# A 4096-cubed matrix product with leaky ReLU: the first unit of k in two runs of 512, A's first run ahead of B, 16-bit transposes

## The chip, the cores and the metric

One core of one Trainium2 chip. The metric is the device time of one execution in microseconds (us); medians are of 4 to 9 executions. "Granted clock" is the share of full speed that the profile records for TensorE. Time ahead of its first record counts as 1.00 in the views and in the mean clock of a run, though the matmuls there start 0.427 us apart, at half pace: a clock of 1.000 says that it did not fall later, not when it became full.

## The reference

```python
def reference(a, b, alpha):          # a, b: 4096 x 4096 float32, alpha 0.01
    x = np.matmul(a, b)
    return np.where(x > 0, x, alpha * x)
```

## The kernel before: the parts that matter

Both operands are rounded to bf16; a matmul multiplies 128 rows of A by 512 columns of B over 128 values of k. 8192 of them are needed. Eight PSUM banks hold four row tiles (`mt`) times two column halves (`nt`). k is cut in four units of 1024; a step is the work on one unit for half of the rows. From the second step on, GpSimd's loads cast while they copy and VectorE turns A. The first unit is special, because nothing has been loaded yet: it comes as fp32 by SP's queue, TensorE transposes A, and ScalarE and VectorE round both operands on the way.

```python
order = [("a", 0), ("b", 0), ("a", 1), ("b", 1), ("a", 2), ("b", 2), ("a", 3)]
order += [("b", c) for c in range(3, kc0)]             # each 512 KB
...
def turn_a(i):
    cols = a_in[:, i, :].rearrange("m (p c) -> m c p", c=kc0)
    for c in range(kc0):                               # 8 fp32 transposes
        nc.tensor.transpose(turned[i, 2 * c // kc0][:, c % (kc0 // 2), :], cols[:, c, :], ident)
    for half, copy in ((0, nc.scalar.copy), (1, nc.vector.tensor_copy)):
        ...                                            # out of PSUM, to bf16
def round_b(i):
    for nt, copy in ((0, nc.scalar.copy), (1, nc.vector.tensor_copy)):
        copy(b0[:, i, columns(nt)], b_in[i][:, columns(nt)])
...
if (what, i) == ("b", 2):                              # lets GpSimd start the next step's loads
    nc.gpsimd.tensor_copy(x[:, :1], b0[:, 2, :1])
```

Ahead of all that, 8 matmuls on zeros ("fillers") run while the first loads are under way, and 2 more after the first tile's transposes.

## Time and profile before

| | before |
|---|---|
| time, median of 6 | 1785.2 us (1784.67 to 1785.49) |
| span of the profile | 1783.2 us |
| TensorE busy | 1768.7 us, 99% (164 matmul records are missing) |
| first real matmul | 6.74 us |
| VectorE's first copy out of a finished bank | 24.79 us |
| last bank's activation starts | 1779.65 us |

How to read it: TensorE is never the idle engine after some 15 us, so the time is the fixed pace of 8192 matmuls plus what is lost ahead of that. VectorE's first copy out of a finished bank tells when the first unit ends; a change in it goes to the end of the kernel one for one unless a later wait takes it up. The profile's lines for this stand in the prediction.

### The profile page before, as it was taken

Reading aid. Unit: us, or ns where it says so; the run is one execution under the profiler, and the core shown is the slowest. Engines: PE = TensorE matmul, PEld = TensorE weight load, DVE = VectorE, ACT = ScalarE, POOL = GpSimd, SP = SyncE. Lnnn points to the kernel's source line nnn. Section 1 sums busy time; section 2 is a strip of 40 time slices with the busy share of each in tenths; the row PEclk is TensorE's granted clock in tenths of the full one; section 3 lists DMA queues with packets and bytes.
Section 4 is the critical chain, followed back from the end, with each engine's and each line's share of the span. In section 5 each row is a group of like instructions: output and inputs, shape, how many; then the busy total and the mean of one; then the engine's idle time right before and its main releaser. Section 6 shows DMA issues by size and latency. Waiting matters only on the chain.

```text
span 1783.2 us, 17975 instructions
## 1 busy us (share of the span) xinstructions
PE 1768.7 (99%) x8070; PEld 806.6 (45%) x8234; DVE 153.4 (9%) x117; ACT 152.0 (9%) x270; POOL 360.1 (20%) x663
## 2 busy tenths in 40 slices
PE   9999999999999999999999999999999999999999
PEld 4444444444444444444444444444444444444444
DVE  4530000032000000002200000000220000000000
ACT  2010000000000000000000000000000000000001
POOL 4630210433002020043201202014320110301000
PEclk9999999999999999999999999999999999999999
DMA  9994653987139165397704917449860481835511
GB/s 260 195 252 108 115 133 86 190 127 125 40 94 189 48 119 118 94 198 128 124 25 96 188 48 142 94 103 202 128 121 12 112 171 48 165 72 121 115 48 47
DMA packets 147020, 214.06 MB, mean 120 GB/s; under 512 B 12800, under 2 KB 76288, under 8 KB 146944
## 3 DMA queue, kind: packets, MB, share of 16 engines
q0 software_dynamic: 126208, 139.50, 48.3%
q10 hardware_dynamic: 18000, 65.54, 9.4%
q1 hardware_dynamic: 2736, 7.87, 1.2%
q8 instruction: 64, 1.05, 0.2%
q14 instruction: 12, 0.10, 0.0%
HBM read 285.21 MB, written 67.11 MB: 198 GB/s over the span
## 4 chain that ended last, share of the span: by engine, by line
PE 99%; issue 1%; DMA 0%; ACT 0%; SPq 0%; DVE 0%
PE ps L154 99%; DMA a_in<-in_a_dram 0%; PE turned L268 0%; DVE at L271 0%; ACT o L384 0%; ACT at L271 0%; SPq L253 0%; SPq L251 0%
## 5 line engine op out<-in xcount | busy, mean ns | idle before, releaser
L154 PE MATMUL ps<-bt,at 128*128 128x512 bf16 x8028 | 1760.5, 379 | 9.3 <-ACT bt L275 0.3
L154 PEld LDWEIGHTS <-at 128*128 128x128 bf16 x8192 | 801.4, 98 | 967.3 <-ACT at L271 1.3
L138 POOL DMA_DIRECT2D bt<-in_b_dram x408 | 217.1, 539 | 1084.7 <-PE ps L154 893.5
L384 ACT ACTIVATE o<-ps 128x512 f32<-128x512 f32 x240 | 130.7, 595 | 1524.5 <-PE ps L154 1450.8
L121 DVE STREAM_TRANSPOSE at<-a 128x1024 uint32<-128x1024 uint32 (+1 forms) x63 | 123.0, 1986 | 1135.7 <-PE ps L154 1113.8
L116 POOL DMA_DIRECT2D a<-in_a_dram x248 | 142.1, 579 | 203.4 <-DVE at L121 140.1
L231 DVE TENSOR_TENSOR part<-ps,part 128x512 f32<-128x512 f32 x32 | 20.4, 686 | 32.6 <-PE ps L154 32.6
L234 ACT ACTIVATE o<-part 128x1024 f32<-128x1024 f32 x8 | 8.5, 1057 | 77.0 <-DVE part L231 64.2
L229 ACT COPY part<-ps 128x512 f32<-128x512 f32 x8 | 4.4, 593 | 15.1 <-PE ps L154 12.3
L227 DVE COPY part<-ps 128x512 f32<-128x512 f32 x8 | 5.2, 679 | 4.8 <-PE ps L154 4.8
L268 PEld LDWEIGHTS turned<-ident,a_in 128*128 128x128 f32 x32 | 4.3, 196 | 2.4 <-issue 1.2
L268 PE MATMUL turned<-ident,a_in 128*128 128x128 f32 x32 | 4.8, 296 | 0.4 <-DMA a_in<-in_a_dram 0.4
L275 ACT CAST bt<-b_in 128x512 bf16<-128x512 f32 x8 | 5.0, 619 | 2.2 <-DMA b_in<-in_b_dram 2.1
L84 PE MATMUL ps<-w 128*128 128x512 bf16 x8 | 3.6, 631 | 1.2 <-DVE x L80 1.2
L275 DVE CAST bt<-b_in 128x512 bf16<-128x512 f32 x8 | 3.4, 432 | 3.8 <-DMA b_in<-in_b_dram 3.8
L271 DVE CAST at<-turned 128x512 bf16<-128x512 f32 x4 | 2.8, 692 | 10.5 <-PE turned L268 10.5
L271 ACT CAST at<-turned 128x512 bf16<-128x512 f32 x4 | 2.3, 585 | 8.7 <-PE turned L268 8.7
L311 POOL CAST x<-bt 128x1 f32<-128x1 bf16 x1 | 0.3, 348 | 11.1 <-ACT bt L275 11.1
L84 PEld LDWEIGHTS <-w 128*128 128x128 bf16 x8 | 1.0, 140 | 2.8 <-issue 1.7
L81 ACT ACT_TABLE_LOAD x1 | 1.3, 1283 | 0.7 <-PEq L406 0.7
L297 PE MATMUL ps<-w 128*128 128x512 bf16 x2 | 0.6, 379 | 0.0
L78 DVE MEMSET w<- 128x256 uint32 x1 | 0.3, 272 | 0.9 <-PEq L406 0.9
(9 smaller groups left out, 1.4 us busy)
## 6 DMA issues: line engine op xcount, KB each, us to landing
bt<-in_b_dram POOLq DMA_DIRECT2D x408, 256.0 KB, 7.9
out_dram<-o ACTq DMA_DIRECT2D x125, 512.0 KB, 3.1
a<-in_a_dram POOLq DMA_DIRECT2D x248, 128.0 KB, 5.2
b_in<-in_b_dram SPq DMA_DIRECT2D x7, 512.0 KB, 10.0
a_in<-in_a_dram SPq DMA_DIRECT2D x4, 512.0 KB, 7.0
out_dram<-o SPq DMA_DIRECT2D x6, 256.0 KB, 2.0
b_in<-in_b_dram SPq DMA_DIRECT2D x2, 256.0 KB, 10.4
```

The source lines that it names most:

```text
L84: nc.tensor.matmul(wp, w[:, :P], w, start=True, stop=True)
L116: nc.gpsimd.dma_start(to, src.rearrange("(g i) w -> i g w", i=32))
L121: nc.vector.transpose(dst.rearrange("p c m e -> p c (m e)").bitcast(U32) .rearrange("p c (g i) -> p g c i", i=32), held[0][:, 4 * t0:4 * t ...
L138: nc.gpsimd.dma_start(new_b(pi, u)[:, c0 + c, :], b_rows(n, s, c))
L154: nc.tensor.matmul(ps, plain(t)[:, c, rows] if (mb, h, u) == (0, 0, 0) else t[:, c // 2, rows, c % 2], bt[pi, u][:, c, nt * NT:(nt + 1) * NT],
L227: nc.vector.tensor_copy(kept, banks[mt, nt])
L231: nc.vector.tensor_add(kept, banks[mt, nt], kept)
L234: nc.scalar.activation(o, part[h][:, mt, :], LRELU, alpha=alpha)
L268: nc.tensor.transpose(turned[i, 2 * c // kc0][:, c % (kc0 // 2), :], cols[:, c, :], ident)
L271: copy(plain(a0)[:, c:c + kc0 // 2, i * P:(i + 1) * P], turned[i, half])
L275: copy(b0[:, i, columns(nt)], b_in[i][:, columns(nt)])
L384: nc.scalar.activation(o[:, cols], banks[mt, nt], LRELU, alpha=alpha)
```

## The change

Its intent: let every chunk of B find all four row tiles of A, so that TensorE gets work faster than chunks land, and make the transposes cheaper. A's first run of 512 k leads in four loads of 256 KB; A's second run comes between B's chunks. VectorE rounds A first, so that transposes are 16-bit. No bank is free for the second run's transposes, so the bank of the last tile and half (`ps7`) is held back for them, and its early products are made up after B's fifth chunk. The next step's A comes in two runs too, and its loads start after B's fourth chunk instead of the third. The last tiles' stores are merged as well. The core of the diff (load helpers, bank tags and bookkeeping are cut):

```diff
-SEGS = [(0, 0, 8), (1, 0, 8), (2, 0, 8), (3, 0, 8)]
+RUNS = [2, 1, 1, 1]
...
-    order = [("a", 0), ("b", 0), ("a", 1), ("b", 1), ("a", 2), ("b", 2), ("a", 3)]
-    order += [("b", c) for c in range(3, kc0)]
+    order = [("a", 0, 0, 1), ("a", 1, 0, 1), ("a", 2, 0, 1), ("a", 3, 0, 1)]
+    order += [("b", 0), ("b", 1), ("b", 2), ("a", 0, 1, 2), ("b", 3), ("a", 2, 1, 2)]
+    order += [("b", c) for c in range(4, KC)]
...
+    def turn_a(i, r, tiles):
+        nc.vector.tensor_copy(a_rounded[:, i:i + tiles, k], a_in[:, i:i + tiles, k])
+        tag = "ps7" if r else f"ps{4 + i}"
+        turned = psum_pool.tile([P, per, tiles, P], BF16, name="turned", tag=tag)
...
+        if r:
+            leaving.append(lambda: nc.vector.tensor_copy(to, turned))
+        else:
+            nc.scalar.copy(to, turned)
...
+            if n < 3:
+                nc.tensor.matmul(wp, w[:, :P], w, start=True, stop=True)
...
-        if (what, i) == ("b", 2):
+        if (what, i) == ("b", 3):
-            nc.gpsimd.tensor_copy(x[:, :1], b0[:, 2, :1])
+            nc.gpsimd.tensor_copy(x[:, :1], b0[:, 3, :1])
+        if (what, i) == ("b", 4):
+            open_bank["late"] = True
+            for c in late:
+                mm0(MT - 1, c, NP - 1)
```

More of the change, by code (lines that the diff above doesn't have):

```diff
@@ L58 @@
     NB = N // RN
-    assert TURNS[0] == [0] and sorted(sum(TURNS, [])) == list(range(len(SEGS)))
-    assert sum(kc for _, _, kc in SEGS) * P == K
-    SEGS_OF = [[s for s in range(len(SEGS)) if SEGS[s][0] == u] for u in range(KU)]
+    KW = KC * P
+    assert TURNS[0] == [0] and sum(TURNS, []) == list(range(KU)) and len(RUNS) == KU
     small_pool = ctx.enter_context(tc.tile_pool(name="small", bufs=1))
@@ L68 @@
     o_pool = ctx.enter_context(tc.tile_pool(name="oo", bufs=2))
-    psum_pool = ctx.enter_context(tc.tile_pool(name="psum", bufs=8, space=bass.MemoryType.PSUM))
-    ident = small_pool.tile([P, P], FP32, name="ident")
+    psum_pool = ctx.enter_context(tc.tile_pool(name="psum", bufs=1, space=bass.MemoryType.PSUM))
+    ident = small_pool.tile([P, P], BF16, name="ident")
     make_identity(nc, ident)
@@ L81 @@
     nc.scalar.activation(x, x, LRELU, alpha=alpha)
-    wp = psum_pool.tile([P, NT], FP32, name="ps")
+    wp = psum_pool.tile([P, NT], FP32, name="wp", tag="ps3")
     for _ in range(8):
@@ L97, in new_b, with load_a @@
         return bt[pi, u]
-    def k_of(s):
-        u, c0, kc = SEGS[s]
-        return (u * KC + c0) * P, kc * P
-    def load_a(mb, h, s, mt, tiles):
-        u, c0, kc = SEGS[s]
-        k0, kw = k_of(s)
+    def load_a(mb, h, u, mt, r):
+        tiles = 2 * RUNS[u]
+        kw = KW // RUNS[u]
+        kc = kw // P
+        k0 = u * KW + r * kw
         row = ((mb * HALVES + h) * MT + mt) * P
@@ L119, in turn @@
         def turn(t0=0, t1=tiles):
-            dst = new_a(mb, h, u)[:, c0 // 2:(c0 + kc) // 2, (mt + t0) * P:(mt + t1) * P, :]
+            rows = slice((mt + t0) * P, (mt + t1) * P)
+            dst = new_a(mb, h, u)[:, r * kc // 2:(r + 1) * kc // 2, rows, :]
             nc.vector.transpose(
@@ L128, in load_a, with b_rows, load_b, pieces_a @@
         return fetch, turn
-    def b_rows(n, s, c):
-        k0, kw = k_of(s)
-        src = b[k0:k0 + kw, n * RN:(n + 1) * RN]
-        return src.rearrange("(p c) n -> p c n", p=P)[:, c, :]
-    def load_b(pi, n, s, c):
-        u, c0, _ = SEGS[s]
-        nc.gpsimd.dma_start(new_b(pi, u)[:, c0 + c, :], b_rows(n, s, c))
-    def pieces_a(mb, h, s, tiles=None):
-        tiles = tiles or 2 * KC // SEGS[s][2]
-        return [load_a(mb, h, s, mt, tiles) for mt in range(0, MT, tiles)]
-    def pieces_b(pi, s):
-        return [lambda c=c: load_b(pi, pairs[pi], s, c) for c in range(SEGS[s][2])]
+    def b_rows(n, u, c):
+        per = KC // RUNS[u]
+        k0 = u * KW + c // per * per * P
+        src = b[k0:k0 + per * P, n * RN:(n + 1) * RN]
+        return src.rearrange("(p c) n -> p c n", p=P)[:, c % per, :]
+    def load_b(pi, n, u, c):
+        nc.gpsimd.dma_start(new_b(pi, u)[:, c, :], b_rows(n, u, c))
+    def pieces_a(mb, h, u):
+        return [load_a(mb, h, u, mt, r) for mt in range(0, MT, 2 * RUNS[u])
+                for r in range(RUNS[u])]
+    def pieces_b(pi, u):
+        return [lambda c=c: load_b(pi, pairs[pi], u, c) for c in range(KC)]
     def plain(t):
@@ L160, in mm, with new_bank @@
         )
+    def new_bank(mt, nt):
+        return psum_pool.tile([P, NT], FP32, name="ps", tag=f"ps{NP * mt + nt}")
     def new_banks():
         return {
-            (mt, nt): psum_pool.tile([P, NT], FP32, name="ps")
+            (mt, nt): new_bank(mt, nt)
             for mt in range(MT)
@@ L188 @@
             lead = 2 if pi == 1 else KU
-            for s in SEGS_OF[u]:
-                loads.setdefault(first * KU + u - lead, []).extend(pieces_b(pi, s))
+            loads.setdefault(first * KU + u - lead, []).extend(pieces_b(pi, u))
     for mb in range(1, MB):
@@ L194 @@
             for u in range(KU):
-                for s in SEGS_OF[u]:
-                    at_slot = first * KU + h * KU + u - 2 * KU + 1
-                    for fetch, turn in pieces_a(mb, h, s):
-                        loads.setdefault(at_slot, []).extend([fetch, turn])
+                at_slot = first * KU + h * KU + u - 2 * KU + 1
+                for fetch, turn in pieces_a(mb, h, u):
+                    loads.setdefault(at_slot, []).extend([fetch, turn])
     def quarter_of(pieces, quarter):
@@ L205 @@
     steps = [
-        (t, h, s, i == 0, i == len(turn) - 1)
+        (t, h, u, i == 0, i == len(turn) - 1)
         for t, turn in enumerate(TURNS)
         for h in range(HALVES)
-        for i, s in enumerate(turn)
+        for i, u in enumerate(turn)
     ]
@@ L214 @@
     turns = []
-    for i, (_, h, s, _, _) in enumerate(steps):
-        made = pieces_a(0, h, s, 2 if i == 1 else None) if i else []
-        fetches.append([fetch for fetch, _ in made] + (pieces_b(0, s) if i and h == 0 else []))
+    for i, (_, h, u, _, _) in enumerate(steps):
+        made = pieces_a(0, h, u) if i else []
+        fetches.append([fetch for fetch, _ in made] + (pieces_b(0, u) if i and h == 0 else []))
         turns.append([turn for _, turn in made])
@@ L235, in spill @@
             nc.scalar.dma_start(place(0, h, pairs[0], mt), o)
-    kw0 = k_of(0)[1]
-    kc0 = SEGS[0][2]
-    a_in = bt_pool.tile([P, MT, kw0], FP32, name="a_in", tag="bt")
-    b_two = [part_pool.tile([P, kc0 // 2, RN], FP32, name="b_in", tag="part") for _ in range(2)]
-    b_in = [b_two[c // 4][:, c % 4, :] for c in range(kc0)]
-    order = [("a", 0), ("b", 0), ("a", 1), ("b", 1), ("a", 2), ("b", 2), ("a", 3)]
-    order += [("b", c) for c in range(3, kc0)]
+    runs = RUNS[0]
+    per = KC // runs
+    rw = per * P
+    assert runs == 2
+    a_rounded = at_pool.tile([P, MT, KW], BF16, name="a_rounded", tag="at")
+    a_in = bt_pool.tile([P, MT, KW], FP32, name="a_in", tag="bt")
+    b_two = [part_pool.tile([P, KC // 2, RN], FP32, name="b_in", tag="part") for _ in range(2)]
+    b_in = [b_two[c // 4][:, c % 4, :] for c in range(KC)]
+    order = [("a", 0, 0, 1), ("a", 1, 0, 1), ("a", 2, 0, 1), ("a", 3, 0, 1)]
+    order += [("b", 0), ("b", 1), ("b", 2), ("a", 0, 1, 2), ("b", 3), ("a", 2, 1, 2)]
+    order += [("b", c) for c in range(4, KC)]
+    HALVED = (KC - 1,)
     def columns(nt):
         return slice(nt * NT, (nt + 1) * NT)
-    for what, i in order:
+    for what, i, *more in order:
         if what == "a":
-            nc.sync.dma_start(a_in[:, i, :], a[i * P:(i + 1) * P, :kw0])
-        elif i < kc0 - 1:
+            r, tiles = more
+            k = slice(r * rw, (r + 1) * rw)
+            src = a[i * P:(i + tiles) * P, k].rearrange("(t p) k -> p t k", p=P)
+            nc.sync.dma_start(a_in[:, i:i + tiles, k], src)
+        elif i not in HALVED:
             nc.sync.dma_start(b_in[i], b_rows(pairs[0], 0, i))
@@ L258 @@
     b0 = new_b(0, 0)
-    turned = {
-        (i, half): psum_pool.tile([P, kc0 // 2, P], FP32, name="turned", tag="ps")
-        for i in range(MT)
-        for half in range(2)
-    }
-    def turn_a(i):
-        cols = a_in[:, i, :].rearrange("m (p c) -> m c p", c=kc0)
-        for c in range(kc0):
-            nc.tensor.transpose(turned[i, 2 * c // kc0][:, c % (kc0 // 2), :], cols[:, c, :], ident)
-        for half, copy in ((0, nc.scalar.copy), (1, nc.vector.tensor_copy)):
-            c = half * kc0 // 2
-            copy(plain(a0)[:, c:c + kc0 // 2, i * P:(i + 1) * P], turned[i, half])
+    leaving = []
+    def turn_a(i, r, tiles):
+        k = slice(r * rw, (r + 1) * rw)
+        nc.vector.tensor_copy(a_rounded[:, i:i + tiles, k], a_in[:, i:i + tiles, k])
+        tag = "ps7" if r else f"ps{4 + i}"
+        turned = psum_pool.tile([P, per, tiles, P], BF16, name="turned", tag=tag)
+        cols = a_rounded[:, :, k].rearrange("m t (p c) -> m t c p", c=per)
+        for t in range(tiles):
+            for c in range(per):
+                nc.tensor.transpose(turned[:, c, t, :], cols[:, i + t, c, :], ident)
+        to = plain(a0)[:, r * per:(r + 1) * per, i * P:(i + tiles) * P]
+        turned = turned.rearrange("p c t m -> p c (t m)")
+        if r:
+            leaving.append(lambda: nc.vector.tensor_copy(to, turned))
+        else:
+            nc.scalar.copy(to, turned)
     def round_b(i):
@@ L275, in round_b @@
             copy(b0[:, i, columns(nt)], b_in[i][:, columns(nt)])
+        for leave in leaving:
+            leave()
+        leaving.clear()
     there = {"a": [], "b": []}
     waiting = []
-    begun = set()
+    late = []
     banks = {}
-    def work():
-        for mt, c in waiting:
-            for nt in range(NP):
-                mm(banks[mt, nt], 0, 0, 0, 0, mt, nt, c, (mt, nt) not in begun, False)
-                begun.add((mt, nt))
-        waiting.clear()
-    for n, (what, i) in enumerate(order):
-        if what == "a":
-            turn_a(i)
+    open_bank = {"late": False}
@@ new lines, in mm0, with work @@
+    def mm0(mt, c, nt, stop=False):
+        if (mt, nt) == (MT - 1, NP - 1) and not open_bank["late"]:
+            late.append(c)
+            return
+        started = (mt, nt) in banks
+        if not started:
+            banks[mt, nt] = new_bank(mt, nt)
+        mm(banks[mt, nt], 0, 0, 0, 0, mt, nt, c, not started, stop)
+    def work(keep=0):
+        now = waiting[:len(waiting) - keep]
+        del waiting[:len(now)]
+        for nt in range(NP):
+            for mt, c in now:
+                mm0(mt, c, nt)
@@ L293 @@
+    for n, (what, i, *more) in enumerate(order):
+        if what == "a":
+            r, tiles = more
+            turn_a(i, r, tiles)
+            if n < 3:
+                nc.tensor.matmul(wp, w[:, :P], w, start=True, stop=True)
+            work()
+            there["a"] += [(i + t, r) for t in range(tiles)]
+            waiting += [(i + t, c) for t in range(tiles) for c in there["b"] if c // per == r]
         else:
             round_b(i)
-        if n == 0:
-            for _ in range(2):
-                nc.tensor.matmul(wp, w[:, :P], w, start=True, stop=True)
-            banks = new_banks()
@@ L299 @@
-        work()
-        there[what].append(i)
-        if what == "a":
-            waiting += [(i, c) for c in there["b"]]
-        elif n < len(order) - 1:
-            waiting += [(mt, i) for mt in there["a"]]
-            kept = waiting.pop() if len(waiting) > 1 else None
-            work()
-            if kept:
-                waiting.append(kept)
-        if (what, i) == ("b", 2):
-            nc.gpsimd.tensor_copy(x[:, :1], b0[:, 2, :1])
-        if n == len(order) - 1:
-            part[0] = part_pool.tile([P, MT, RN], FP32, name="part", tag="part")
@@ L314 @@
-    waiting += [(mt, kc0 - 1) for mt in there["a"]]
+            work()
+            there["b"].append(i)
+            waiting += [(mt, i) for mt, r in there["a"] if i // per == r]
+            if n < len(order) - 1:
+                work(keep=1)
+        if (what, i) == ("b", 3):
[4 more added lines that the diff above has]
+                mm0(MT - 1, c, NP - 1)
+    part[0] = part_pool.tile([P, MT, RN], FP32, name="part", tag="part")
@@ L318 @@
         for mt, c in waiting:
-            mm(banks[mt, nt], 0, 0, 0, 0, mt, nt, c, False, True)
+            mm0(mt, c, nt, stop=c == KC - 1)
     turns[1][0](0, 1)
@@ L324 @@
             turns[1][0](1, 2)
+    turns[1][0](2, 4)
     turns[1][1]()
@@ L329 @@
     for i in range(1, len(steps)):
-        t, h, s, first, last = steps[i]
-        u, c0, kc = SEGS[s]
-        head = 0 if h else kc // 2 if last else kc
+        t, h, u, first, last = steps[i]
+        head = 0 if h else KC // 2 if last else KC
         groups = [([(mt, c) for c in range(head) for mt in range(MT)], None)]
-        groups += [([(mt, c) for c in range(head, kc)], mt if last else None) for mt in range(MT)]
+        if i == 1:
+            head = KC // RUNS[u]
+            groups = [([(mt, c) for mt in range(MT) for c in range(head)], None)]
+        groups += [([(mt, c) for c in range(head, KC)], mt if last else None) for mt in range(MT)]
         following = turns[i + 1] if i + 1 < len(steps) else []
-        if len(following) == 1:
-            where = [2]
-        else:
-            where = [0, 3]
+        where = [0, 3]
         own = 2 * KU - 2 + i - (len(steps) - 2)
@@ L355 @@
                 for nt in range(NP):
-                    mm(banks[mt, nt], 0, h, 0, u, mt, nt, c0 + c, first and c == 0,
-                       last and c == kc - 1)
+                    mm(banks[mt, nt], 0, h, 0, u, mt, nt, c, first and c == 0,
+                       last and c == KC - 1)
             for piece, turn in enumerate(following):
@@ L384 @@
                         nc.scalar.activation(o[:, cols], banks[mt, nt], LRELU, alpha=alpha)
-                        if final and mt:
+                        if final and mt == MT - 1:
                             nc.sync.dma_start(to[:, cols], o[:, cols])
-                    if not final or mt == 0:
+                    if not final or mt < MT - 1:
                         nc.scalar.dma_start(to, o)
```

## The prediction

> **What bounds the kernel now.** I read the page first (engine shares, the chain that ended last, the groups), then the timeline of the first 40 us and of the last 10, then the issue and landing times of the DMAs. The page says that TensorE is the bound, and that one line of the kernel is nearly the whole chain:
>
> ```profile
> span 1783.2 us, 17975 instructions
> ...
> PE 1768.7 (99%) x8070; PEld 806.6 (45%) x8234; DVE 153.4 (9%) x117; ACT 152.0 (9%) x270; POOL 360.1 (20%) x663
> ...
> PE 99%; issue 1%; DMA 0%; ACT 0%; SPq 0%; DVE 0%
> ...
> L154 PE MATMUL ps<-bt,at 128*128 128x512 bf16 x8028 | 1760.5, 379 | 9.3 <-ACT bt L275 0.3
> L154 PEld LDWEIGHTS <-at 128*128 128x128 bf16 x8192 | 801.4, 98 | 967.3 <-ACT at L271 1.3
> L268 PE MATMUL turned<-ident,a_in 128*128 128x128 f32 x32 | 4.8, 296 | 0.4 <-DMA a_in<-in_a_dram 0.4
> ```
>
> The reader is to see two things. The product takes 8192 matmuls (the weight loads count them; 164 matmul records are missing). And 379 ns is the latency of one, not its pace: in the chain in order of time, stretches begin at 23.87 and at 34.66 us and hold 50 matmuls, so the pace is 10.79 / 50 = 0.2158 us. 8192 x 0.2158 = 1767.9 us that the change doesn't touch. The rest of the span is 1783.2 - 1767.9 = 15.3 us, and it lies at the two ends. The last bank's activation starts at 1779.65, so 3.55 us are the way out of the last tile; about 11.7 us are lost at the front. TensorE's timeline shows where:
>
> ```profile
> 4.58 1.41 PE L268 MATMUL turned<-ident,a_in 128*128 128x128 f32 x8
> 5.83 0.59 PE L297 MATMUL ps<-w 128*128 128x512 bf16 x2
> 6.74 0.75 PE L154 MATMUL ps<-bt,at 128*128 128x512 bf16 x2 [0.32 <-ACT bt L275]
> 7.84 1.16 PE L268 MATMUL turned<-ident,a_in 128*128 128x128 f32 x8 [0.36 <-DMA a_in<-in_a_dram]
> 9.23 0.94 PE L154 MATMUL ps<-bt,at 128*128 128x512 bf16 x3 [0.23 <-ACT at L271]
> 9.79 0.70 PE L154 MATMUL ps<-bt,at 128*128 128x512 bf16 x2
> 10.49 1.13 PE L268 MATMUL turned<-ident,a_in 128*128 128x128 f32 x8
> 11.46 2.11 PE L154 MATMUL ps<-bt,at 128*128 128x512 bf16 x9
> 13.62 1.05 PE L268 MATMUL turned<-ident,a_in 128*128 128x128 f32 x8
> 14.51 25.71 PE L154 MATMUL ps<-bt,at 128*128 128x512 bf16 x115
> ```
>
> The first real matmul is at 6.74; then three batches of fp32 transposes and small waits for A and B alternate with matmuls; from about 15.4 on the starts follow each other at 0.2158 us with no gap to the end. By the moment at which the first unit's banks come free (DVE's first copy out at 24.79), I put the end of the first unit (64 matmuls, 13.8 us of work) at 25.2 us. So **the quantity to predict is this one**: 25.2 - 13.8 = 11.4 us of front, and any stall that the change makes right after it.
>
> **What the Trainium skill says.** "TensorE: Matmul & The Clock Gate", section on the back-to-back gap, gives 215.7 ns for 512 columns at the full clock: the trace agrees (215.8). The same page, in "Why this matters for your kernels", warns of idle gaps over some 3 us, after which the clock halves; the page's granted clock is full from 5.3 us, and nothing in this trace shows a fall. "DMA: Bandwidth & Descriptors", Specifications, asks for at least 512 B per transfer for line rate. The DMA packet records agree as far as they go: 4096 B packets take about 161 ns, 2048 B ones 93 ns (so 12 to 16% more per byte), 512 B ones on the software queue 60 ns with overlap; smaller data packets do not occur. "VectorE: DVE Perf Modes", tier table, allows at most double rate for a PSUM source; the fp32 copies here (512 elements in 0.69 us) run at single rate, and no 16-bit one occurs.
>
> **The change, part by part.**
>
> 1. *Order of loads.* Before, A tile, B chunk, A tile, B chunk, each 512 KB, landed at 4.4, 5.6, 7.8, 9.1 and then every 1.28 us. Now four half-length A tiles of 256 KB come ahead of the first B chunk: 1.5 MB instead of 1 MB must land before the first product, and A's rows become 2 KB packets. Working from the landings: third slot 7.8, plus 0.1 to 0.4 for the smaller packets, is B0 at about 7.9 to 8.2 (7.1 if the 0.9 us that the third landing lost is not lost again). ACT's cast takes 0.62, so the first real matmul comes at about 8.5 (7.9 to 8.9) instead of 6.74. **Cost: about +1.8 us.**
>
> 2. *Transposes.* 32 of fp32, 0.111 us apart when warm, become 32 of bf16, which I put at 0.055 to 0.08. Before, 24 of them stood among the matmuls (2.7 us); now 16 do (0.9 to 1.3), the first 16 fall into the wait for B0. **Gain: 1.4 to 1.8 us.** The new rounding of A on DVE costs 0.42 us for 512 columns (as B's cast) and about 0.69 for 1024, beside TensorE.
>
> 3. *Work per chunk.* Once four A tiles are there, each B chunk brings 8 matmuls, 1.73 us, against 1.28 us to land it. Before, the first chunks brought 2, 4, 10, and TensorE waited. Of the 11.4 us of front, 6.74 is before the first product and 2.7 are transposes, so about 1.9 are waits. Now I walk the chunks: 8.6 first product; B0, B1, B2 give seven each (one bank is withheld) to 12.9 without a wait; A's second run 12.0 + 0.69 rounding, transposes to 13.4; B3 lands about 13.3, cast by 13.95, wait 0.2, done 15.3; A's other half lands 14.75, rounded by 15.45, wait 0.3, transposed and left over by 16.4; B4 lands 16.0, cast by 16.65, wait 0.3; its third tile waits 0.1 more for DVE's copy out of the last bank. 36 matmuls are left and chunks come faster than work: 36 x 0.2158 = 7.8, **end of the unit near 24.6**. If the 0.9 us is not lost, 23.9. The waits now sum to 0.9, **gain about 1.0**. Together: +1.8 - 1.6 - 1.0 = -0.8, and I take 24.4 against 25.2.
>
> 4. *The withheld bank.* Its four early matmuls are done after B4; the number of matmuls is the same. No cost unless DVE's copy (about 0.67 us at double rate, 1.2 at single) is late.
>
> 5. *The next step's A.* GpSimd starts its loads when B3 is rounded instead of B2: 14.0 against 12.4. These too are cut in two runs, so the packets written become 256 B. Before, four issues from 12.67 landed by 22.08 and DVE turned the first tile at 22.20, with 1.5 us to spare before the first copy out:
>
> ```profile
> 22.20 1.10 DVE L121 STREAM_TRANSPOSE at<-a 128x512 uint32<-128x512 uint32 x1 [0.93 <-DMA a<-in_a_dram]
> 24.79 0.69 DVE L227 COPY part<-ps 128x512 f32<-128x512 f32 x1 [1.48 <-PE ps L154]
> 25.39 1.10 DVE L121 STREAM_TRANSPOSE at<-a 128x512 uint32<-128x512 uint32 x1
> 26.42 1.85 DVE L227 COPY part<-ps 128x512 f32<-128x512 f32 x3
> ```
>
> Now 1 MB from about 18.0 (software packets came 4 us after issue), beside the last 0.3 MB of B, at 400 GB/s and 1.4 us to land, is 22.7; with packets up to half as efficient, 25.1. A quarter-size turn is about 0.67 us, and the copy that frees the second bank stands behind it on DVE. With a landing at 23.4: turned 24.1, bank freed 24.7, wanted at about 24.6. Later the third and fourth tiles' turn stands behind three copies (1.85 us) and ends near 28.2, wanted near 28.0. **Cost: about 0.4 us, from 0.1 to 1.6.** Unit 1's loads landed before by 40.2 where the last was wanted near 50: slack enough.
>
> 6. *Tail.* Only the last tile is still stored in halves by SP; two others go out whole on ACT's queue, ended 1.7 us and more before the last. 3.55 us as before.
>
> Sum: -0.8 + 0.4 = -0.4; for the parts that I cannot size I lean a little towards the intent of the change: **-0.6 us, 1784.5**.
>
> **The rivals.**
> A. *The front shrinks by over a microsecond*: the third landing's loss doesn't come again and small packets cost nothing. For it: no byte was missing in those microseconds, so it may be one engine's accident. Time about 1783.5.
> B. *The next step's A takes the wait over*: 256 B packets land late and TensorE stalls at 24 to 26 us. For it: the spare of 1.5 us is spent twice, by the later trigger and the earlier end of the unit; against it: the records show packet time nearly proportional to size from 2048 to 512 B. Time 1785 to 1786.3.
> C. *The clock falls*: between the transposes and the first product TensorE has about 1.2 us of work in 3.4. One window at half clock would cost up to 1.7 us. Against it: three filler matmuls were put there, and the gaps are short. About one in ten; 1786.
> D. *Hidden anyway*: 8128 of the 8192 matmuls are untouched, so all of these end within 0.1% of the old time.
>
> **Range and chances.** Parts 1 to 3 leave 23.8 to 25.0 for the end of the unit, part 5 adds 0.1 to 1.6: from -1.3 to +1.4 us, and three runs of the kernel before spread over 0.8. That gives 1783.2 to 1786.2. A change of 2% is 36 us, three times the whole front: within 2% is as good as certain.
>
> **What would show it.** First real matmul near 8.5; seven matmuls per chunk at full pace from there; waits near 14, 15.5 and 16.5; the unit's last product near 24.4; the first turn of the next step's A near 24 and a gap in TensorE's starts there or near 28 shorter than 0.6; nothing after 35 us changed; tail 3.5 us. Wrong would be: a first landing of B well before 7.5, a granted clock below 1 after 5.3, a stall over 1 us at the second step, or any gap in the later regions.

## The result, and the profile after

| | before | after |
|---|---|---|
| time, median of 6 | 1785.2 us (1784.67 to 1785.49) | 1787.4 us (1785.22 to 1788.73) |
| span of the profile | 1783.2 | 1784.6 |
| mean granted clock of the profile | 1.000 | 0.999 |
| first real matmul | 6.74 | 9.75 |
| VectorE's first copy out | 24.79 | 26.00 |
| last activation starts | 1779.65 | 1781.01 |

The ratio of the times is 1.0011 (95% interval 0.9998 to 1.0024). No difference is shown with certainty, but the change did not help, and its runs scatter over 3.5 us where those of before scatter over 0.8. The six runs of after list their mean clock: 1.000 for the run of 1785.22, 0.999 for the four of 1786.34 to 1787.82, 0.998 for the one of 1788.73.

From the page of the changed kernel, the lines that answer to those of before:

```profile
span 1784.6 us, 18140 instructions
...
PE 1777.1 (100%) x8235; PEld 805.4 (45%) x8235; DVE 144.7 (8%) x122; ACT 152.1 (9%) x270; POOL 363.8 (20%) x663
...
L152 PE MATMUL ps<-bt,at 128*128 128x512 bf16 x8192 | 1770.5, 379 | 1.3 <-ACT bt L288 1.2
...
L278 PE MATMUL turned<-ident,a_rounded 128*128 128x128 bf16 x32 | 3.3, 245 | 1.4 <-DVE a_rounded L272 1.4
```

They show little: the transposes are cheaper (3.3 us busy for 4.8). That TensorE looks busy for longer says nothing, because the trace of before lacks 164 matmul records and this one has all 8192. Where the time goes, TensorE's timeline shows (start, duration, instructions, count, idle time before and what ended it):

```profile
6.19 0.39 PE L278 MATMUL turned<-ident,a_rounded 128*128 128x128 bf16 x4
6.42 0.38 PE L323 MATMUL wp<-w 128*128 128x512 bf16 x1
8.15 0.41 PE L278 MATMUL turned<-ident,a_rounded 128*128 128x128 bf16 x4 [1.35 <-DVE a_rounded L272]
9.75 6.02 PE L152 MATMUL ps<-bt,at 128*128 128x512 bf16 x20 [1.19 <-ACT bt L288]
15.61 0.61 PE L278 MATMUL turned<-ident,a_rounded 128*128 128x128 bf16 x8
```

Two things are to be seen. The fourth A tile's transposes wait until 8.15, and the first product until 9.75: loads are late. And 20 matmuls fill 6.02 us, where 20 x 0.2158 = 4.3. The table of stretches shows it (stretch, length, busy time of PE, PEld, DVE, ACT and POOL with counts, then granted clock, DMA share and GB/s). First the changed kernel, cut at the moments at which its granted clock changes:

```profile
6.08:9.50 3.42, 1.13 (x10) 0.56 (x9) 0.85 (x2) 2.00 (x4) 0.00 (x0) 1.00 1.00 365
9.50:12.91 3.41, 3.16 (x8) 1.14 (x8) 0.89 (x3) 1.44 (x3) 0.00 (x0) 0.50 1.03 410
12.91:16.32 3.41, 3.41 (x23) 1.78 (x22) 1.15 (x3) 0.62 (x1) 1.53 (x3) 1.00 1.05 408
```

Then the kernel before, in stretches of the same 3.41 us from the moment at which its clock became full:

```profile
5.32:8.73 3.41, 2.74 (x18) 1.68 (x16) 1.02 (x2) 1.24 (x3) 0.00 (x0) 1.00 1.02 400
8.73:12.14 3.41, 3.18 (x19) 1.64 (x18) 1.50 (x3) 1.93 (x4) 0.00 (x0) 1.00 1.02 412
```

In the changed kernel TensorE worked for 1.13 of 3.42 us, and the next 3.41 us ran at half clock: 8 matmuls instead of some 15. In the kernel before it worked for 2.74 of 3.41 and kept the clock. The stretch's length is that of the activity window in the Trainium skill, "TensorE: Matmul & The Clock Gate", Part 1 (3413 ns, free-running); the trace agrees with 3.413 us. Because the window starts at no fixed moment of the kernel, the same program can fall or not fall (in two profiles of one program, e5_bfirst_warm and e11_bfirst_again below, the clock becomes full at 4.38 and at 6.53 us): that fits clocks of 1.000, 0.999 and 0.998 (none, one or two half-clock windows, 3.413 x 0.5 / 1784 = 0.001 each).

VectorE's lines for the end of the unit, changed kernel: the turn of the next step's A, then the first copy out.

```profile
24.94 0.45 DVE L119 STREAM_TRANSPOSE at<-a 128x256 uint32<-128x256 uint32 x1 [2.30 <-DMA a<-in_a_dram]
25.07 2.05 ACT L228 COPY part<-ps 128x512 f32<-128x512 f32 x4 [3.65 <-PE ps L152]
25.10 0.58 POOL L113 DMA_DIRECT2D a<-in_a_dram  x1 [0.20 <-issue]
26.00 0.69 DVE L226 COPY part<-ps 128x512 f32<-128x512 f32 x1 [0.61 <-PE ps L152]
```

The turn is done 0.6 us ahead of the copy. TensorE's starts show one gap of 0.15 us at 26.4, and none after it: from there 8127 matmuls follow each other at 0.2158 us, the pace of before. So the whole loss of this profile lies at the front: 1.21 us up to the first copy out, and that gap. The profiled run, 1786.34 us, is the second fastest of the six: its span is 1.4 us longer than that of before, where the medians differ by 2.2.

The landings, from the issue and landing times in the trace (us):

| | 1st | 2nd | 3rd | 4th | 5th | B's fifth chunk |
|---|---|---|---|---|---|---|
| before | A 4.41 | B 5.64 | A 7.80 | B 9.10 | A 10.36 | 15.49 |
| after | A 3.70 | A 4.34 | A 4.97 | A 7.64 | B 8.88 | 16.70 |

After, the first three come 0.63 apart and the fourth 2.67 later, 2.0 too late. So there are two suspects: the clock, and late loads.

### The profile page after: what moved, and what is told of

Same layout as the page of the kernel before. It is cut to its first block, busy times and chain, and to the rows that moved or that the text cites. A ratio compares the mean times of both kernels' runs of the same rounds, so it can differ in the third digit from the quotient of the medians.

```text
span 1784.6 us, 18140 instructions
## 1 busy us (share of the span) xinstructions
PE 1777.1 (100%) x8235; PEld 805.4 (45%) x8235; DVE 144.7 (8%) x122; ACT 152.1 (9%) x270; POOL 363.8 (20%) x663
## 4 chain that ended last, share of the span: by engine, by line
PE 99%; DMA 0%; ACT 0%; SPq 0%; DVE 0%; issue 0%
PE ps L152 99%; DMA a_in<-in_a_dram 0%; PE turned L278 0%; SPq L259 0%; DVE at L282 0%; ACT o L411 0%; ACT at L284 0%; ACT bt L288 0%; DVE a_rounded L272 0%
## 5 line engine op out<-in xcount | busy, mean ns | idle before, releaser
L119 DVE STREAM_TRANSPOSE at<-a 128x1024 uint32<-128x1024 uint32 (+2 forms) x64 | 112.2, 1785 | 1153.3 <-DMA a<-in_a_dram 595.3
L113 POOL DMA_DIRECT2D a<-in_a_dram x248 | 145.9, 593 | 197.7 <-DVE at L119 131.9
L84 PE MATMUL wp<-w 128*128 128x512 bf16 x8 | 3.6, 631 | 1.2 <-DVE x L80 1.2
L323 PE MATMUL wp<-w 128*128 128x512 bf16 x3 | 1.5, 502 | 0.0
```

Of the source, the lines that this page charges most:

```text
L84: nc.tensor.matmul(wp, w[:, :P], w, start=True, stop=True)
L113: nc.gpsimd.dma_start(to, src.rearrange("(g i) w -> i g w", i=32))
L119: nc.vector.transpose(dst.rearrange("p c m e -> p c (m e)").bitcast(U32) .rearrange("p c (g i) -> p g c i", i=32), held[0][:, 4 * t0:4 * t ...
```

## The experiments

**Does the clock cost the time? (e1_fill, e2_nofill)** e1_fill puts fillers where TensorE idled, e2_nofill takes the three away.

```diff
-            if n < 3:
+            for _ in range({0: 1, 1: 1, 2: 7, 3: 6}.get(i, 0) if r == 0 else 0):   # e1_fill
                 nc.tensor.matmul(wp, w[:, :P], w, start=True, stop=True)           # e2_nofill: both lines gone
```

> The changed kernel with 9 more throw-away matmuls on zeros, 6 ahead of the last A tile's transposes and 6 (instead of none) between them and the first product, so that TensorE is not idle from 6.4 to 9.75 us. Theory 1 (the granted clock falls to 0.5 for one 3.4 us window because TensorE was busy for only 1.1 us of the window before): mean clock 1.000 in every run, no half-clock window, the unit ends about 1.2 us earlier than in the changed kernel's profile, time 1785.2 within 0.4 and with the spread of the kernel before (under 1 us). Theory 2 (only the late landings of A and B count, the clock is incidental): 1787, as the changed kernel, first product at 9.75 still.

Measured: 1786.31 us (1785.51 to 1786.76), before in the same rounds 1785.06. Its profile, in stretches, then VectorE's first copy out:

```profile
5.00:8.40 3.40, 2.83 (x22) 1.42 (x22) 0.85 (x2) 1.56 (x3) 0.00 (x0) 1.00 0.89 279
8.40:11.80 3.40, 3.39 (x18) 1.45 (x16) 0.98 (x3) 1.95 (x4) 0.00 (x0) 1.00 1.03 408
...
25.17 0.69 DVE L226 COPY part<-ps 128x512 f32<-128x512 f32 x1 [0.16 <-PE ps L152]
```

Full clock from 4.3 us, first product still at 9.77, and the copy out comes at 25.17 instead of 26.00. (The stretches shown do not start with a window. The window from 4.31 to 7.73 is busy for 3.18 of 3.42 us.) So the clock is a cause: 0.8 us in the profiles, 1.0 in the difference to the kernel before (+1.25 instead of +2.2; separate rounds, whose intervals overlap). But the expected 1785.2 was missed: with the clock at 1.000 in all five runs the change still costs over a microsecond in the medians. Against that stands the one run of the changed kernel at 1.000, which took 1785.22, the time of before.

> The changed kernel without its three filler matmuls: even less work for TensorE between 5 and 9.7 us. Theory 1: the clock falls in every run, perhaps for two windows: mean clock 0.998 to 0.999 always, 1787 to 1789. Theory 2: the fillers lie beside waits, so 1787 as the changed kernel and no shift in clock.

Measured: 1787.52 us (1786.21 to 1788.09). The profile's stretches:

```profile
4.46:7.87 3.41, 1.28 (x13) 0.74 (x11) 0.86 (x2) 1.66 (x3) 0.00 (x0) 1.00 0.95 276
7.87:14.70 6.83, 5.15 (x15) 2.08 (x16) 2.44 (x6) 2.38 (x5) 0.00 (x0) 0.50 1.04 408
```

1.28 us of work, then two windows at half clock (6.83 us), and the copy out at 27.17. The runs list the same: 0.998 for 1787.52, 1787.53 and 1788.09 us, 0.999 for 1786.21. So the clock fell in every run, mostly for two windows, and the median lies where theory 1 put it; theory 2 expected no shift in clock. That the median is no worse than that of the changed kernel (1787.4) speaks for neither: four runs that scatter over 1.9 us do not tell the two apart. What carries the clock's part is its record run by run and the profiles, not the medians.

**Why are the loads late? (e3_touch, e7_rows)** In the changed kernel the DMA traffic has a hole at 5 to 7 us: 0.47 MB where the kernel before moved 0.77, with single packets of over 1 us as B's first chunk begins. A first touch of B seemed possible. e3_touch reads a little of those rows first; e7_rows reads the first chunk from neighbouring rows.

```diff
+    touch = small_pool.tile([P, P], FP32, name="touch")                # e3_touch, on e1_fill
+    nc.sync.dma_start(touch, b_rows(pairs[0], 0, 0)[:, :P])
...
+        elif i == 0:                                                   # e7_rows, on e1_fill
+            nc.sync.dma_start(b_in[i], b[:P, :RN])
```

> As e1_fill, with one small load (64 KB) of the rows of B's first chunk issued ahead of everything, into a tile that nobody reads. Theory 3a (the hole in the DMA traffic at 5 to 7 us, after which the fourth A tile lands at 7.64, is the price of the first touch of B, which the kernel before paid during its start-up): no packets near 1 us when B0 begins, the fourth A tile lands at 6.4 to 6.8, first product near 8.7, time 1784.2. Theory 3b (the hole comes with that moment or with that load, whatever was touched before): fourth A tile at 7.6 to 7.9, 1785.2 as e1_fill.

Measured: 1786.52 us (1786.1 to 1787.23); fourth A tile at 7.60, B's first chunk at 9.36, packets of up to 2 us as B began. The hole moved along with the start of B's load (from 4.8 to 5.4 us), and a touch of 64 KB did not take it away: theory 3a, as it was tested, falls.

> e1_fill with B's first chunk read from 128 neighbouring rows (2 MB of B) instead of every fourth row of 512 (8 MB); the result is wrong on purpose. Theory 3c (the hole at 5 to 7 us comes from the scattered rows of that first load): fourth A tile lands at 6.4 to 6.8 and B's first chunk near 7.9, time about 1 us below e1_fill. Theory 3d (the hole comes with the start of B's stream in that moment, whatever its rows): fourth A tile at 7.5 or later, time as e1_fill, 1786.

Measured: 1785.82 us (1785.58 to 1786.77) against 1784.97 for before; fourth A tile at 7.99, B's first chunk at 9.25. Theory 3c falls too.

**The order of loads (e4_bfirst, e5_bfirst_warm)**

```diff
-    order = [("a", 0, 0, 1), ("a", 1, 0, 1), ("a", 2, 0, 1), ("a", 3, 0, 1)]
-    order += [("b", 0), ("b", 1),
+    order = [("b", 0), ("a", 0, 0, 1), ("a", 1, 0, 1), ("a", 2, 0, 1), ("a", 3, 0, 1)]
+    order += [("b", 1),
...
-    for _ in range(8):                    # e5_bfirst_warm: 12 at the start, none after the transposes
+    for _ in range(12):
```

> The changed kernel with B's first chunk loaded ahead of the four A tiles; the same bytes before the fifth landing, fillers only the original three. Theory 3a: the fourth A tile lands near 7.0, first product near 6.5 to 7.1, TensorE has work from then on, so the clock stays at 1.000, and later chunks come about 0.9 us earlier: 1784.3. Theory 3b: the fourth A tile lands at 8 or later, later chunks come as in the changed kernel, clock 1.000, 1785.1.

Measured: 1785.23 us (1784.9 to 1785.35), before 1785.06. The fourth A tile landed at 7.81, B's fifth chunk at 15.64 instead of 16.70: the same bytes in another order are a microsecond earlier. Against the expectation the clock was not full from the start: the matmuls up to 10.1 us follow each other at 0.427 us, half the pace. TensorE had idled from 4.8 to 5.9 us, and the window from 3.52 to 6.93 us, busy for 2.34 of 3.41 us, did not raise the clock.

```profile
5.85 0.62 PE L278 MATMUL turned<-ident,a_rounded 128*128 128x128 bf16 x4 [1.07 <-DVE a_rounded L272]
```

> e4_bfirst with 12 throw-away matmuls at the start instead of 8 and none between the transposes. In e4_bfirst the profile shows the half clock until 10.3 us, because TensorE was idle from 4.8 to 5.9 us and its first window was not full. Theory 1 (the granted clock follows how full TensorE was, and early half-clock work delays everything after it): full clock from about 5 to 8 us, the unit ends near 24.3 instead of 25.5, time 1784.0, about 1 us below the kernel before. Rival (the chunks' landings set the end of the unit whatever the clock did before 10 us): 1785.1, as e4_bfirst.

Measured: 1784.59 us (1784.37 to 1784.83), before 1784.97 (1784.61 to 1785.68). Full clock from 4.4 us; first copy out at 24.00 against 24.79 in the kernel before and 25.00 in e4_bfirst. The direction is that of the clock's theory; of the expected microsecond below before, some 0.4 came. A second series of the same program:

> The same program as e5_bfirst_warm, to see whether its small gain over the kernel before (1784.59 against 1784.97) comes back: 1784.6 within 0.4 and below the median of the kernel before by 0.2 to 0.8 if it is real; no difference or the other sign if it was chance.

Measured: 1784.6 us (1784.15 to 1785.02), before 1785.26 (1785.02 to 1785.79). The small gain came back (each interval of the ratio reaches over 1). In this profile the clock was full from 6.53 only and the first copy out still came at 23.77, with landings 0.2 us earlier, so half clock up to 6.5 us cost nothing that can be seen here.

**The cheaper transposes alone (e6_before_bf16, e8_bf16_fill)** The kernel before with its own order, but A rounded first and transposed in 16 bits; then the same with fillers that add zero onto an open bank.

```diff
+        nc.vector.tensor_copy(a_rounded[:, i, :], a_in[:, i, :])
-        cols = a_in[:, i, :].rearrange("m (p c) -> m c p", c=kc0)
+        cols = a_rounded[:, i, :].rearrange("m (p c) -> m c p", c=kc0)
...
+        for _ in range({1: 8, 2: 2}.get(n, 0)):                        # e8_bf16_fill only
+            nc.tensor.matmul(banks[0, 0], w[:, :P], w, start=False, stop=False)
```

> The kernel before, its order of loads untouched, with only the rounding of A on VectorE and the 16-bit transposes of the change. The prediction counted 1.4 to 1.8 us for the transposes. If TensorE's own work is what fills the first 15 us, the unit ends 1 us earlier and the time is 1784.1. If the waits for A and B stand behind the transposes, most of it turns into longer waits, and the added rounding (0.7 us per tile) eats the rest: 1785.0 within 0.4. Clock full from about 5 us in either case.

Measured: 1786.28 us (1784.59 to 1786.46), before 1784.97. Cheaper transposes made the kernel slower in four of five runs, and these four list a clock of 0.999, the fast one 1.000, as do all runs of the kernel before beside the experiments. Its profile:

```profile
4.04:7.46 3.42, 2.12 (x14) 0.83 (x12) 1.45 (x3) 1.10 (x2) 0.00 (x0) 1.00 1.00 334
7.46:10.87 3.41, 1.30 (x12) 0.82 (x12) 1.45 (x3) 1.10 (x2) 0.00 (x0) 1.00 0.98 357
10.87:14.28 3.41, 3.41 (x15) 1.52 (x14) 2.07 (x4) 1.10 (x2) 0.65 (x2) 0.50 1.03 418
```

2.12 us of work in a window kept the clock, 1.30 lost it for the next. The second A tile also landed later in this profile (8.41 against 7.80), so part of the idle time is not the transposes'.

> e6_before_bf16 (order of before, 16-bit transposes) with 10 matmuls on zeros, added onto an open bank, in the waits for the second A tile. In e6_before_bf16 TensorE was busy for 1.30 of 3.41 us from 7.46 to 10.87 and the next window ran at half clock; four of its five runs took 1785.9 to 1786.5 and one 1784.59. Theory 1 (cheaper transposes take away work that had kept the clock up; half clock costs 1.2 to 1.8 us): full clock in the profile, median 1784.6 within 0.4 and no run above 1785.3. Rival (16-bit transposes with their rounding are slower on the path themselves, whatever the clock): 1786.2 as e6_before_bf16.

Measured: 1785.08 us (1784.86 to 1785.28), before 1784.84. Clock full, no run above 1785.3. Ten matmuls that compute nothing brought back 1.1 us (+0.24 over the kernel before instead of +1.31). And with the clock held the cheaper transposes are worth nothing that can be measured here. That their time turned into waits for the loads fits, but no run shows it apart.

**Trying to shorten the waits inside the unit (e9_best, a miss)** A's second run earlier, its bank emptied at once. Also changed, and cut below: the withheld matmuls come before B's fourth chunk, and the next step's loads start after its third.

```diff
-    order += [("b", 1), ("b", 2), ("a", 0, 1, 2), ("b", 3), ("a", 2, 1, 2)]
+    order += [("b", 1), ("a", 0, 1, 2), ("b", 2), ("a", 2, 1, 2), ("b", 3)]
...
-            leaving.append(lambda: nc.vector.tensor_copy(to, turned))
+            nc.vector.tensor_copy(to, turned)
```

> e5_bfirst_warm with A's second run loaded between B1 and B2 and between B2 and B3 instead of around B3, its bank emptied at once, the withheld matmuls done before B3, and the next step's A loads started after B2. The walk with e5_bfirst_warm's landings: second run transposed by 14.5, bank free near 15.1, from there 40 matmuls without a wait, unit ends near 23.8 against 24.7 in e5_bfirst_warm; first turn of the next step's A near 22.5. Theory (waits inside the unit are what is left): 1783.7. Rival (the last chunks of B, whose landing near 20.9 is pushed out by the earlier loads of A, now set the end): 1784.6, as e5_bfirst_warm.

Measured: 1785.21 us (1784.74 to 1786.14), before 1784.84. TensorE stood still from 14.9 to 15.5 for VectorE's copy out of the held-back bank, with the withheld matmuls in front of work that was ready.

```profile
15.49 20.81 PE L152 MATMUL ps<-bt,at 128*128 128x512 bf16 x93 [0.56 <-DVE at L282]
```

Not the last chunks, but a new wait of the edit's own making: neither theory as written.

**Fewer loads at the start (e10_one_a, e12_bfirst_two_a, e13_start_b2)** e10_one_a is the changed kernel with A's first run in one load of 1 MB, and fillers. e12_bfirst_two_a is e5_bfirst_warm with two loads of 512 KB. e13_start_b2 starts the next step's loads after B2 again.

```diff
+            if r == 0:                     # e12_bfirst_two_a: if i % 2
+                if i:
+                    continue
+                tiles = MT                 # e12_bfirst_two_a: tiles = 2
...
-        if (what, i) == ("b", 3):          # e13_start_b2, on e12_bfirst_two_a
+        if (what, i) == ("b", 2):
```

> The changed kernel with the four A tiles of the first run in one load of 1 MB instead of four of 256 KB, and with fillers (12 at the start, 1, 1, 1 and 5 after the transposes) so that the clock holds. In all profiles so far the landing that falls between 5 and 8 us is late by 0.5 to 2.0 us, most where the ninth load's issue took longest (1.4 to 1.7 us in the A-first kernels). Theory 3f (many small loads queued at once cause it): four loads fewer are queued, A lands complete near 6.1 and B's first chunk near 7.4, first product near 8.1, time 1785.0. Theory 3d (the start of B's stream beside A causes it): B's first chunk still lands at 8.5 to 9.2, first product at 9.3 or later, time 1786.

Measured: 1785.12 us (1785.05 to 1785.35), before 1785.26. The traffic from 5 to 7 us (packets, MB, share of the engines), first of the changed kernel, then of e10_one_a:

```profile
q1 hardware_dynamic: 157, 0.47, 83.6%
```

```profile
q1 hardware_dynamic: 255, 0.85, 104.8%
```

No hole, no packet over 500 ns, every landing on time: A at 6.21, B's chunks at 7.49, 8.77 and 10.05, its fifth at 15.32 instead of 16.70. Theory 3f holds as far as this: without the four small loads at the head, B starts on time. But small loads are not the whole of it. In the kernel before and in e6_before_bf16 every load at the head has 512 KB, and the second A tile still landed 0.9 and 1.4 us late (at 7.80 and 8.41; 1.28 us after B's first chunk would have been 6.92 and 7.00), while e12_bfirst_two_a below has 512 KB loads too and loses nothing. The first product came at 9.78 all the same, because all four tiles are there only at 6.2 and pass VectorE and ScalarE one after the other; that part of the expectation was wrong. With clock and landings put right, the order of the change takes the time of the kernel before.

> e5_bfirst_warm with the four A tiles of the first run in two loads of 512 KB instead of four of 256 KB, so two loads fewer in the first microseconds. In e10_one_a the single load took the delay away: every landing on time, no packet over 500 ns after 3 us. Theory 3f (many small loads at the start cost DMA time): no landing late between 5 and 8 us, B's second chunk near 8.5 instead of 9.2, its fifth near 15.0 instead of 15.7, unit ends near 23.9 instead of 24.7, time 1783.9, about 1.2 us below the kernel before. Rival (the delay comes with the moment and two loads are enough for it, or TensorE's own waits now hold the end): 1784.6, as e5_bfirst_warm.

Measured: 1784.65 us (1784.08 to 1784.95), before 1785.12. No landing was late, and B's chunks came 0.4 us earlier than in e5_bfirst_warm (second 8.79, fifth 15.34), where 0.7 was expected; but there is no gain over e5_bfirst_warm: the rival's time. VectorE's and TensorE's lines at the end of the unit:

```profile
23.98 0.45 DVE L119 STREAM_TRANSPOSE at<-a 128x256 uint32<-128x256 uint32 x1 [3.64 <-DMA a<-in_a_dram]
24.14 0.57 POOL L113 DMA_DIRECT2D a<-in_a_dram  x1 [1.30 <-DMA a<-in_a_dram]
24.35 0.65 DVE L226 COPY part<-ps 128x512 f32<-128x512 f32 x1
...
24.49 0.39 PE L152 MATMUL ps<-bt,at 128*128 128x512 bf16 x1 [0.29 <-DVE at L119]
...
25.06 3.18 PE L152 MATMUL ps<-bt,at 128*128 128x512 bf16 x14 [0.18 <-DVE part L226]
```

The unit is over, but the next step's A has not landed: VectorE idles 3.64 us for it, the copy stands behind the turn, and TensorE waits for both. This is the prediction's part 5, which comes forth in full only when the front is short.

> e12_bfirst_two_a with the next step's A loads started after B2 instead of B3. In e12_bfirst_two_a all landings were on time, yet the time did not fall: TensorE stands at 24.2 to 25.1 us for the turn of the next step's A, whose fourth load landed at 23.86. If that wait is what ate the gain: fourth load lands near 22, turned before 23, no gap at the start of the second step, time 1784.0. Rival (the earlier loads of A push B's last chunks out and the first unit ends later by as much): 1784.6, as e12_bfirst_two_a.

Measured: 1784.17 us (1784.14 to 1784.64), before 1785.06 (1784.27 to 1785.76). The fourth of those loads landed at 23.51 instead of 23.86, the turn at 23.63, so the wait shrank and did not go (near 22 and before 23 were expected). This version is the fastest, 0.9 us below the kernel before in the medians; the interval of its ratio (0.9982 to 1.0009) reaches over 1, so it is a small gain seen in one series.

## Why the prediction was wrong

1784.5 was predicted (1783.2 to 1786.2), 1787.4 was measured. "Within 2%" was right, as it had to be for a change in 11 us of 1785.

- **The step that failed is rival C, put at about one in ten because "three filler matmuls were put there, and the gaps are short".** The walk of parts 1 to 3 ran at full clock all the way. The prediction had the right sum (about 1.2 us of work in 3.4; 1.13 measured) and the right cost (up to 1.7 us), and misjudged what it does. No gap was over 1.4 us, and the clock fell in five of the six runs, once probably twice. The gaps being short was taken as safety; the busy share of the window told more: after 33 to 38% the clock fell (after, e2_nofill, e6_before_bf16), after 62% and more it stayed (62 in e6_before_bf16, 68 in e10_one_a, 80 in before). Held by fillers, it gives back 1.0 us of the 2.2.
- **Part 1 was mis-sized.** B's first chunk was to land at 7.9 to 8.2 and did so at 8.88; the first product was to come at 8.5 and came at 9.75. The prediction knew the 0.9 us that the third landing lost before, and let it come back at most once; it came back as 2.0. e10_one_a points to it for the remainder of the loss: from +1.25 us with the clock held to -0.14 with the loads merged (and the fillers placed otherwise). Of the first product's delay the late landing is one part only: ScalarE, still copying the fourth tile out, began B's cast 0.2 us after the landing.
- **Part 2, the transposes.** The size was right: 0.056 us apart when warm, 0.107 when cold, against an estimate of 0.055 to 0.08. The mistake was to book 1.4 to 1.8 us as gain: e8_bf16_fill shows none, and e6_before_bf16 shows that the removed work had helped to keep the clock.
- **Part 3, work per chunk,** was right in its start: from the first product on, 20 matmuls follow without a wait. The waits that it put near 14, 15.5 and 16.5, 0.9 us in sum, did not come in this form: after 3.2 us of slow matmuls TensorE was behind the loads, and its one wait up to the end of the unit is 0.3 us at 18.7. At half clock the order buys little. (The walk has a slip too: 21 matmuls from 8.6 us end at 13.1, not at 12.9.)
- **Part 4** was right on the copy: 1024 16-bit columns in 0.69 us, where 512 of fp32 take as long, so double rate. But the wait of 0.3 us just named is for this copy, where 0.1 was put.
- **Part 5, the next step's A,** was right in mechanism and too large: 0.15 us for 0.4, because the unit ended late. What the 256 B packets cost stays open. The first four loads took 9.9 us from the first issue to the last landing against 9.4 before; all eight landed within 6.5 us of each other against 4.9, but within 4.5 in e1_fill, which has the same packets. And the records did not show packet time "nearly proportional" to size: on the software queue 2048 B took 173 ns and 512 B 60.
- **Part 6, the tail,** was right: 3.6 us for 3.55.
- **A citation.** The 215.7 ns stands in the Trainium skill, "TensorE: Matmul & The Clock Gate", under "Step-by-step". The section "Back-to-back issue gap" gives some 131 ns for a sustained stream; the trace has 215.8.

What stays open: the mechanism of the late landing between 5 and 8 us, which in smaller form was in the kernel before too; and why three other runs of e1_fill are 0.8 to 1.2 us longer than the profiled one. Their clock of 1.000 does not tell when it became full, so a later start of the full clock, or later loads, could each be it.

## What to carry to other kernels

Before taking work from TensorE ahead of a dense stretch, count its busy share in windows of 3.4 us: work that looks like overhead can be what keeps the clock, and matmuls on zeros in the waits cost nothing that these runs could measure. When reordering loads at a kernel's start, compare landings, not bytes: the same bytes in four loads or one differed by a microsecond. And when a front gets shorter, look at once at what was started relative to it.

## What the Trainium skill lacked or had wrong

- "TensorE: Matmul & The Clock Gate", Part 1 and "Why this matters for your kernels": it warns of idle gaps of some 3 us, and tells of many short idle times as a second way to lose the clock, but gives no busy share. Here the clock halved for 3.41 us with no gap over 1.35 us, after a window with 1.13 of 3.42 us busy, and again after 1.28 and 1.30 of 3.41; 2.12 of 3.42 and 2.74 of 3.41 kept it.
- The same page, Part 4 (PE-mode transpose), says that transposes do not count as busy in the same way. In the kernel before, fp32 transposes were 1.56 of the 2.74 busy us of the window that kept the clock. Without them 1.18 of 3.41 us are left, a share at which other windows lost it. That speaks against the page for fp32; no run separates it.
- The same page gives no share for the way up either. With TensorE idle from 4.8 to 5.9 us after 3.6 us of fillers, e4_bfirst ran at half clock until 10.3 us: 2.34 of 3.41 us busy (69%) did not raise the clock, though 62% kept it in e6_before_bf16.
- "DMA: Bandwidth & Descriptors", Specifications: 512 B as the least size for line rate; that row has no size for the loss. In the first 35 us 256 B packets on the software queue took 53 ns on the mean and 512 B ones 64 in the changed kernel, 42 and 60 in e5_bfirst_warm, so 1.4 to 1.6 times as long per byte; the landings do not settle what that costs.
- "DMA: Bandwidth & Descriptors" has general advice for large transfers, but nothing on landings that come late at a kernel's start: with four loads of 256 KB at the head 0.47 MB moved from 5 to 7 us, with one load of 1 MB 0.85 MB, and with the 512 KB loads of before and e6_before_bf16 0.77 and 0.65 MB.
